# Feed-forward weight sums by VectorE and by accumulating transfers, and a fixed order for the last products, in a two-layer encoder trunk

## The chip, the cores and the metric

The kernel runs on one core of a Trainium2 chip. The metric is the device time of one execution in microseconds (us); lower is better. The shown time of a kernel is the median of several executions. A separate execution was taken with the hardware profiler; all rows below come from it.

## The reference

256 rows of 1024 channels (float32) pass through two layers. Each layer adds a half feed-forward, a mixer and another half feed-forward to the running rows `h`; the mixer is a convolution module in layer 0 and latent attention in layer 1. A final norm follows.

```
h += 0.5 * ((silu(n(h) @ w1) * (n(h) @ w3)) @ w2)     # n = RMSNorm; w1, w3: 1024 x 2816, w2: 2816 x 1024
h += mixer(n(h))                                      # layer 0: GLU, conv of width 31, norm, silu, product
h += 0.5 * ((silu(n(h) @ v1) * (n(h) @ v3)) @ v2)     # layer 1's mixer: low-rank q/k/v, rotary keys, softmax
```

So there are four feed-forwards, F0 to F3: two in the convolution layer and two in the attention layer. Each reads 33 MB of weights, and their products fill most of the time.

## The kernel before, in words

**Precision and weight blocks.** Products are made from pairs: a float32 matrix is split into a rounded high part `hi` and a remainder `lo`, and three matrix instructions (`mm3`: high x low, high x high, low x high) add up in PSUM. Weights come in blocks of 128 x 2048 (1 MB, one transfer on SyncE's queue into a `raw` buffer). For each block ScalarE writes `hi` (a cast) and VectorE writes `lo` (`raw - hi`), in two pieces of 1024 columns (`PIECES = 2`). There are four `raw` buffers and four `hi`/`lo` pairs, used in turn; a block may be cast once the pair's previous block has been used by TensorE. `weights()` hands out the next block and sees to it that the following ones are loaded ahead.

**A feed-forward.** `ffn_in` first makes the up-projection: six column groups c of 512 columns (the last is half as wide), 22 blocks. `turn` transposes each result through a DRAM buffer (`gd`, `gb`) and splits it into `Gh`, `Gl`. Then `Rows` makes the down-projection with 11 blocks ("units" 0 to 10) into four PSUM banks `o[tb, d]`: tb is the half of the rows (128 each), d the half of the 1024 columns. Units 0, 2, 4, 6 and 8 (`FAST`) are made by a Strassen-like scheme with 7 products in place of 8, so 21 matrix instructions in place of 24. It needs four sums of quarters of the weight block (`load_fast`: the first two by GpSimd at L172, two by VectorE at L173 and L174), which take a second `raw` buffer and a second `hi`/`lo` pair, and sums of quarters of the activations (`combine`: four subtractions by GpSimd, L611). Four of the seven products gather in shared banks p1, q6, p5, q7. After unit 8 `fold` adds these to `h`, with GpSimd doing the four additions to `h` (L552, L555, L557, L559). `finish` then takes units 9 and 10: per bank 12 matrix instructions, an addition of the bank to `h` (L566) and what the next stage can begin: `Plain` (in front of the convolution) or `Norm` (elsewhere) makes sums of squares on ScalarE (L298), a power on GpSimd, transposes on TensorE and the split of the normed rows into `Xh`, `Xl`. These two tiles lie idle from the end of an up-projection to the end of that feed-forward.

**What sets the order.** Every engine takes its instructions in a fixed order that a planner makes from a simulated timeline; instructions traced inside an `urgent` function go first, and `behind` puts a cast after the last six urgent instructions of its engine that were traced before it. In `finish` the last six products in front of the convolution wait, by an ordering (`after = nxt.turned`), behind the transposes of the first half of the rows; for `Norm` the list `turned` is empty.

Of the kernel before, what the change touches and what calls it, by code (L numbers as in the profile page):

```python
# [19 lines left out]
P = 128  # L20
D = 1024
# [24 lines left out]
FAST = (0, 2, 4, 6, 8)  # L46
# [34 lines left out]
def trunk(ctx: ExitStack, tc: tile.TileContext, x, xt, pos, invf, gains, gfin, wdw,  # L81
# [28 lines left out]
    for i in range(2):  # L110
        for w13, w2 in ((f1w13, f1w2), (f2w13, f2w2)):

            for cc_ in range(5):
                for m in range(2):
                    blocks += [w13[i, m, 2 * cc_ + a_] for a_ in range(2)]
            blocks += [w13[i, a_, 10] for a_ in range(2)]
            blocks += [("fast", w2[i, a_]) if a_ in FAST else w2[i, a_] for a_ in range(NF // 2)]
# [26 lines left out]
    def load(src, pieces=1):  # L144
        if isinstance(src, tuple) and src[0] == "fast":
            return load_fast(src[1])
# [12 lines left out]
        for i in range(pieces):  # L159
            c = slice(i * n // pieces, (i + 1) * n // pieces)  # L160
            behind(nc.scalar.copy(hi[:, c], raw[:, c]))  # L161
            behind(nc.vector.tensor_sub(lo[:, c], raw[:, c], hi[:, c].bitcast(F32)))  # L162
        return hi, lo

    def load_fast(src):

        raw = rawp.tile([P, HB], F32, tag="raw", name=uid("raw"))
        sums = rawp.tile([P, HB], F32, tag="raw", name=uid("sums"))
        nc.sync.dma_start(raw, src)
        v = raw.rearrange("p (b n) -> p b n", n=512)  # L170
        t = sums.rearrange("p (b n) -> p b n", n=512)
        behind(nc.gpsimd.tensor_tensor(t[:, 0:2, :], v[:, 0:4:3, :], v[:, 1:2, :].to_broadcast([P, 2, 512]), op=ALU.add))  # L172
        behind(nc.vector.tensor_add(t[:, 2, :], t[:, 0, :], v[:, 3, :]))  # L173
        behind(nc.vector.tensor_add(t[:, 3, :], t[:, 2, :], v[:, 2, :]))  # L174
        out = []
        for x, cols in ((raw, ((0, 512), (1024, 2048))), (sums, ((0, 1024), (1024, 2048)))):
            hi = wp.tile([P, HB], F32R, tag="hi", name=uid("hi"))
            lo = wp.tile([P, HB], F32R, tag="lo", name=uid("lo"))
            for c0, c1 in cols:
                behind(nc.scalar.copy(hi[:, c0:c1], x[:, c0:c1]))  # L180
                behind(nc.vector.tensor_sub(lo[:, c0:c1], x[:, c0:c1], hi[:, c0:c1].bitcast(F32)))  # L181
            out.append((hi, lo))
# [18 lines left out]
    def load_ahead(ahead=W_BUFS - 2):  # L201
# [4 lines left out]
        load_to(b)  # L206

    def load_to(last):
        while len(loaded) < last:
            loaded.append(load(blocks[len(loaded)], PIECES))  # L210

    def weights(n=1, more=True, ahead=W_BUFS - 2):
        out = []
        for _ in range(n):
            n_used[0] += 1
            if more:
                load_ahead(ahead)
# [117 lines left out]
    class Norm:  # L335


        def __init__(self, gname, half=False):
# [7 lines left out]
            self.turned = ()  # L346
# [152 lines left out]
    class Rows:  # L499
        def __init__(self, zh, zl, nk, last=False, sh=None, sl=None):  # L500
# [4 lines left out]
            self.early = max(i for i in range(nk // 2 - 2) if sh is None or i not in FAST)  # L505
# [6 lines left out]
        def mm(self, part, i, tb, d, o, key, f1, o0=0, o1=512, after=()):  # L512
            hi, lo = part
            for j in range(2):
                f = 2 * i + j
                c = slice(j * D + d * 512 + o0, j * D + d * 512 + o1)
                mm3(o, self.zh[:, f, tbs(tb)], self.zl[:, f, tbs(tb)], hi[:, c], lo[:, c], self.begin(key),
                    f == f1 - 1, after)
# [8 lines left out]
        def fast(self, i):  # L527

            n = FAST.index(i)
# [6 lines left out]
            for o, key, (ah, al), (hi, lo), q in (  # L536
                    (self.p[0], "p1", z(f, 0), raw, 0), (self.o[0, 0], (0, 0), z(f + 1, 0), raw, 2),
                    (self.o[0, 1], (0, 1), s(2), raw, 3), (self.p[2], "p5", z(f, 1), sums, 0),
                    (self.p[3], "q7", s(1), sums, 1), (self.p[1], "q6", s(0), sums, 2),
                    (self.o[1, 0], (1, 0), z(f + 1, 1), sums, 3)):  # L540
                c = slice(q * 512, q * 512 + 512)
                mm3(o, ah, al, hi[:, c], lo[:, c], self.begin(key), isinstance(key, str) and i == FAST[-1])
            if i == FAST[-1]:
                self.fold()

        def fold(self):
# [748 lines left out]
```

## Time and profile before

| | |
|---|---|
| median of 3 runs | 933.74 us (932.46 to 934.13) |
| profiled execution | 930.08 us, span 928.3 us |
| TensorE busy | 913.5 us (98%), clock 0.998 |
| VectorE / ScalarE / GpSimd busy | 687.6 / 536.4 / 213.4 us |
| DMA | 191.58 MB, mean 206 GB/s |

A profile row names a line, an engine, the operation and the tiles (`out<-in`), then how often it ran, its busy time, the mean of one and the idle time in front of it. In a timeline the first two columns are the start and the duration in us, and square brackets hold the idle time in front with what ended it. A windows view gives, for a stretch of time, its length and the busy time of TensorE, its weight loads, VectorE, ScalarE and GpSimd (instructions in brackets), then the clock, the DMA share and GB/s. PE is TensorE, DVE is VectorE, ACT is ScalarE, POOL is GpSimd, SP is SyncE.

### The profile page before, as it was taken

Reading aid. Unit: us, or ns where it says so; the run is one execution under the profiler, and the core shown is the slowest. Engines: PE = TensorE matmul, PEld = TensorE weight load, DVE = VectorE, ACT = ScalarE, POOL = GpSimd, SP = SyncE. Lnnn points to the kernel's source line nnn. Section 1 sums busy time; section 2 is a strip of 40 time slices with the busy share of each in tenths; the row PEclk is TensorE's granted clock in tenths of the full one; section 3 lists DMA queues with packets and bytes.
Section 4 is the critical chain, followed back from the end, with each engine's and each line's share of the span. In section 5 each row is a group of like instructions: output and inputs, shape, how many; then the busy total and the mean of one; then the engine's idle time right before and its main releaser. Section 6 shows DMA issues by size and latency. Waiting matters only on the chain.

```text
span 928.3 us, 12409 instructions
## 1 busy us (share of the span) xinstructions
PE 913.5 (98%) x4337; PEld 761.0 (82%) x4337; DVE 687.6 (74%) x1047; ACT 536.4 (58%) x928; POOL 213.4 (23%) x325
## 2 busy tenths in 40 slices
PE   9999999899999999999999999999999999999997
PEld 7888888798977888888888888888898778888886
DVE  5777787889974667778876667878666476667975
ACT  6964465558865445455575445655667374544643
POOL 1110222349931001222210003223200010003223
PEclk9999999999999999999999999999999999999999
DMA  9986555823323866565857765657451557774651
GB/s 340 348 291 231 203 170 216 317 90 139 137 91 127 299 243 237 184 196 198 308 198 237 246 233 184 193 206 262 181 182 46 182 204 236 254 246 150 226 181 46
DMA packets 60399, 191.58 MB, mean 206 GB/s; under 512 B 11184, under 2 KB 33328, under 8 KB 40752
## 3 DMA queue, kind: packets, MB, share of 16 engines
q1 hardware_dynamic: 59760, 190.09, 58.7%
q8 instruction: 34, 0.56, 0.2%
q10 hardware_dynamic: 576, 0.69, 0.2%
q14 instruction: 29, 0.24, 0.1%
HBM read 178.17 MB, written 12.58 MB: 205 GB/s over the span
## 4 chain that ended last, share of the span: by engine, by line
PE 89%; DVE 5%; ACT 3%; DMA 1%; issue 1%; SPq 0%; POOLq 0%; ACTq 0%; POOL 0%; DVEq 0%
PE u L275 17%; PE u L271 17%; PE u L274 17%; PE o L271 6%; PE o L274 6%; PE o L275 6%; DVE lo L162 3%; PE u L717 3%; PE gate L717 3%; PE p L275 2%; PE p L271 2%; PE p L274 2%; PE o L901 2%; PE y L790 2%; ACT hi L161 1%
## 5 line engine op out<-in xcount | busy, mean ns | idle before, releaser
L162 DVE TENSOR_TENSOR lo<-raw,hi 128x1024 fp32r<-128x1024 f32 (+1 forms) x250 | 304.9, 1255 | 76.9 <-ACT hi L161 76.8
L161 ACT CAST hi<-raw 128x1024 fp32r<-128x1024 f32 (+1 forms) x250 | 248.0, 1046 | 153.3 <-PE u L275 111.1
L275 PE MATMUL u<-hi,Xl 128*128 128x512 f32 x688 | 267.8, 390 | 0.7 <-DVE Xl L330 0.7
L271 PE MATMUL u<-lo,Xh 128*128 128x512 f32 x688 | 268.1, 390 | 0.1
L274 PE MATMUL u<-hi,Xh 128*128 128x512 f32 x688 | 267.7, 389 | 0.0
L275 PEld LDWEIGHTS u<-hi,Xl 128*128 128x128 f32 x688 | 129.2, 188 | 28.5 <-DVE Xl L330 1.6
L271 PEld LDWEIGHTS u<-lo,Xh 128*128 128x128 f32 x688 | 129.2, 188 | 26.8 <-DVE lo L162 0.5
L274 PEld LDWEIGHTS u<-hi,Xh 128*128 128x128 f32 x688 | 129.2, 188 | 26.8
L271 PE MATMUL o<-lo,Gh 128*128 128x512 f32 (+1 forms) x236 | 91.0, 386 | 0.0
L275 PE MATMUL o<-hi,Gl 128*128 128x512 f32 (+1 forms) x236 | 91.0, 385 | 0.0
L274 PE MATMUL o<-hi,Gh 128*128 128x512 f32 (+1 forms) x236 | 91.0, 385 | 0.0
L172 POOL TENSOR_TENSOR sums<-raw 128x1024 f32<-128x1024 f32 x20 | 53.1, 2653 | 161.2 <-DMA raw<-in_f2w 52.6
L611 POOL TENSOR_TENSOR sx<-gb 128x128 f32<-128x128 f32 x20 | 10.4, 521 | 311.9 <-DMA gb<-gd 311.9
L181 DVE TENSOR_TENSOR lo<-sums,hi 128x1024 fp32r<-128x1024 f32 x40 | 56.1, 1433 | 0.0
L603 ACT CAST Gh<-gb 128x512 fp32r<-128x512 f32 (+2 forms) x48 | 25.6, 539 | 49.8 <-DMA gb<-gd 49.6
L761 DVE SCALAR_TENSOR_TENSOR acc<-V,dw,acc 128x256 f32<-128x256 f32 (+1 forms) x160 | 54.0, 417 | 0.1
L180 ACT CAST hi<-sums 128x1024 fp32r<-128x1024 f32 x40 | 40.7, 1052 | 22.5 <-PE u L275 15.3
L604 DVE TENSOR_TENSOR Gl<-gb,Gh 128x512 fp32r<-128x512 f32 (+2 forms) x48 | 33.1, 704 | 26.4 <-ACT Gh L603 26.4
L275 PEld LDWEIGHTS o<-hi,Gl 128*128 128x128 f32 x236 | 44.3, 188 | 9.0
L274 PEld LDWEIGHTS o<-hi,Gh 128*128 128x128 f32 x236 | 44.3, 188 | 9.0
L271 PEld LDWEIGHTS o<-lo,Gh 128*128 128x128 f32 x236 | 44.3, 188 | 8.7
L180 ACT CAST hi<-raw 128x512 fp32r<-128x512 f32 (+1 forms) x40 | 31.4, 834 | 34.7 <-PE o L275 27.8
(246 smaller groups left out, 1336.6 us busy)
## 6 DMA issues: line engine op xcount, KB each, us to landing
raw<-in_f2w SPq DMA_DIRECT2D x66, 1024.0 KB, 4.8
raw<-in_f1w SPq DMA_DIRECT2D x64, 1024.0 KB, 5.3
raw<-in_cw SPq DMA_DIRECT2D x12, 1024.0 KB, 6.0
gd<-gt SPq DMA_DIRECT2D x160, 64.0 KB, 2.5
gb<-gd SPq DMA_DIRECT2D x40, 256.0 KB, 3.0
raw<-in_wo SPq DMA_DIRECT2D x4, 1024.0 KB, 4.9
raw<-in_wuq SPq DMA_DIRECT2D x3, 1024.0 KB, 4.7
raw<-in_f1w SPq DMA_DIRECT2D x8, 256.0 KB, 6.2
```

The source lines that it names most:

```text
L161: behind(nc.scalar.copy(hi[:, c], raw[:, c]))
L162: behind(nc.vector.tensor_sub(lo[:, c], raw[:, c], hi[:, c].bitcast(F32)))
L172: behind(nc.gpsimd.tensor_tensor(t[:, 0:2, :], v[:, 0:4:3, :], v[:, 1:2, :].to_broadcast([P, 2, 512]), op=ALU.add))
L180: behind(nc.scalar.copy(hi[:, c0:c1], x[:, c0:c1]))
L181: behind(nc.vector.tensor_sub(lo[:, c0:c1], x[:, c0:c1], hi[:, c0:c1].bitcast(F32)))
L271: mm = nc.tensor.matmul(o, ah, bl, start=start, stop=False)
L274: nc.tensor.matmul(o, ah, bh, start=False, stop=False)
L275: return nc.tensor.matmul(o, al, bh, start=False, stop=stop)
L603: nc.scalar.copy(dh, x)
L604: nc.vector.tensor_sub(dl, x, dh.bitcast(F32))
L717: mm = nc.tensor.matmul(u[:, t], w[:, c], X.x[:, k, t], start=(k == 0), stop=(k == KT - 1))
L761: nc.vector.scalar_tensor_tensor(out if j == j1 - 1 else y, v, w, y, op0=ALU.mult, op1=ALU.add)
```

## The change

- The weight blocks of a feed-forward other than those of its first column group are cast in one piece of 2048 columns ("wide"); fast blocks in pieces of 1536 (the quarter that is not used directly comes last in a new block layout) and 2048.
- The first two weight sums of units 0 and 2 go from GpSimd to one VectorE instruction. For units 4, 6 and 8 two transfers on GpSimd's queue make them: the last quarter is written twice, then the first two quarters are added by an accumulating transfer. They land in the space of `Xh` (units 4 and 8) and `Xl` (unit 6).
- `combine` goes to VectorE; the activation difference is made in place.
- `fold` is urgent and on VectorE; its half for the second rows is a new `fold_second`, traced after the second bank's addition. In unit 8 the four shared products come first.
- In `finish` the products have a fixed order (banks 0 and 1: unit 9 for both, then unit 10), each group behind the one before. The casts of the second block of the next stage are held until the second bank's addition has been traced (not in F0; in the attention's `finish` too). `Norm.turned` now holds the transposes of the first rows, so the last six products wait for them there as well.

```
-            blocks += [w13[i, a_, 10] for a_ in range(2)]
-            blocks += [("fast", w2[i, a_]) if a_ in FAST else w2[i, a_] for a_ in range(NF // 2)]
+                    blocks += [("wide", w13[i, m, 2 * cc_ + a_]) if cc_ else w13[i, m, 2 * cc_ + a_]
+                               for a_ in range(2)]
+            blocks += [("wide", w13[i, a_, 10]) for a_ in range(2)]
+            blocks += [("fast" if a_ in FAST[2 * i + g_] else "wide", w2[i, a_]) for a_ in range(NF // 2)]
...
+        casts() if later is None else later.append(casts)
...
+    def start_sums(b, tag):
+        src = blocks[b][1]
+        sums = xp.tile([P, HB], F32, tag=tag, name=uid("sums"))
+        t = sums[:, :1024].rearrange("p (b n) -> p b n", n=512)
+        nc.gpsimd.dma_start(t, src[:, 1536:].unsqueeze(1).to_broadcast([P, 2, 512]))
+        nc.gpsimd.dma_start(sums[:, :1024], src[:, :1024], accum_op=ALU.add)
+        sums_of[b] = sums
...
-        behind(nc.gpsimd.tensor_tensor(t[:, 0:2, :], v[:, 0:4:3, :], v[:, 1:2, :].to_broadcast([P, 2, 512]), op=ALU.add))
-        behind(nc.vector.tensor_add(t[:, 2, :], t[:, 0, :], v[:, 3, :]))
+        if sums is None:
+            sums = rawp.tile([P, HB], F32, tag="raw", name=uid("sums"))
+            t = sums.rearrange("p (b n) -> p b n", n=512)
+            nc.sync.dma_start(raw, src)
+            behind(nc.vector.tensor_add(t[:, 0:2, :], v[:, 0:2, :], v[:, 3:4, :].to_broadcast([P, 2, 512])))
+        else:
+            t = sums.rearrange("p (b n) -> p b n", n=512)
+            nc.sync.dma_start(raw[:, :1536], src[:, :1536])
+        behind(nc.vector.tensor_add(t[:, 2, :], t[:, 0, :], v[:, 1, :]))
         behind(nc.vector.tensor_add(t[:, 3, :], t[:, 2, :], v[:, 2, :]))
...
-        for x, cols in ((raw, ((0, 512), (1024, 2048))), (sums, ((0, 1024), (1024, 2048)))):
+        for x, n in ((raw, 1536), (sums, HB)):
...
         def part(self, tb, q, after=(), low_after=()):
             split_rows(h[tb], 4 * q, 4, self.col, self.xh, self.xl, tb, after, low_after,
-                       self.between if tb == 1 else None)
+                       self.between if tb == 1 else self.turned)
...
+            if end:
+                order_ = [shared[0], shared[3], shared[1], shared[2], *own]
+            else:
+                order_ = [shared[0], *own[:2], *shared[1:], own[2]]
...
+        @urgent
         def fold(self):
...
-            nc.gpsimd.tensor_tensor(h[0][:, left], h[0][:, left], s1, op=ALU.add)
...
+            nc.scalar.copy(s1, p1)
+            nc.vector.tensor_add(h[0][:, :512], p1, h[0][:, :512])
+            nc.vector.tensor_sub(self.v, q6, s1)
+            nc.vector.tensor_add(self.w, p5, self.v)
+            nc.vector.tensor_add(h[0][:, 512:], h[0][:, 512:], self.w)
+
+        @urgent
+        def fold_second(self):
+            for c, x, op in ((slice(0, 512), self.v, ALU.subtract), (slice(512, D), self.w, ALU.add)):
+                y = tmp.tile([P, 512], F32, tag="s", name=uid("fold"))
+                nc.vector.tensor_add(y, self.p[3], x)
+                nc.vector.tensor_tensor(h[1][:, c], h[1][:, c], y, op=op)
...
-            parts = weights(2)
+            later = []
+            parts = weights(1) + weights(1, later=later if hold else None)
...
+            steps = [(n, a) for n in range(len(pieces)) for a in range(2)]
+            if self.units:
+                steps[:4] = [(0, 0), (1, 0), (0, 1), (1, 1)]
+            before = None
+            for n, a in steps:
+                i, tb, d, o0, o1, o, key = pieces[n]
+                after = [before] if before is not None and self.units else []
+                if i == 3 and a == 1 and not self.last:
+                    after += nxt.turned
+                before = self.mm(parts[a], nb - 2 + a, tb, d, o, key, self.nk, o0, o1, after)
...
+                if i == 1:
+                    while later:
+                        later.pop()()
+                if i == 1 and self.units:
+                    self.fold_second()
...
-            sub(v[:, 3], b1[:, 0], b1[:, 1])
...
+                nc.vector.tensor_sub(s7, a21, a11)
+                nc.vector.tensor_sub(a21, a21, a22)
+                nc.vector.tensor_sub(s6, a11, a21)
+                nc.vector.tensor_sub(s3, a12, s6)
...
         for i in range(NF // 2 - 2):
-            (o.fast if i in FAST else o.block)(i)
+            for n, at, tag in ((2, 0, "Xh"), (3, 0, "Xl"), (4, units[2], "Xh")):
+                if i == at:
+                    start_sums(first_block + units[n], tag)
+            (o.fast if i in units else o.block)(i)
             beside()
-        return o.finish(make_next, act)
+        return o.finish(make_next, act, X.whole is False)
```

More of the change, by code (lines that the diff above doesn't have):

```diff
@@ L205, in load_ahead, with load_to, weights @@
             b += 1
-        load_to(b)
-    def load_to(last):
+        load_to(b, later)
+    def load_to(last, later=None):
         while len(loaded) < last:
-            loaded.append(load(blocks[len(loaded)], PIECES))
-    def weights(n=1, more=True, ahead=W_BUFS - 2):
+            loaded.append(load(blocks[len(loaded)], PIECES, later))
+    def weights(n=1, more=True, ahead=W_BUFS - 2, later=None):
         out = []
```

162 lines of the change are left out of this document (80 added, 82 removed).

## The prediction

> **What bounds the kernel now.** I read the page's busy shares, then the waits of TensorE, then windows around the places that these name. TensorE is busy 98% of the span; what it waits for is a list of single places.
>
> ```profile
> PE 913.5 (98%) x4337; PEld 761.0 (82%) x4337; DVE 687.6 (74%) x1047; ACT 536.4 (58%) x928; POOL 213.4 (23%) x325
> PE tp L433 <- ACT sigm L422: 2.9, 1, 2.9
> PE u L275 <- DVE Xl L330: 0.7, 2, 0.4
> 127.24 0.39 PE L271 MATMUL p<-lo,Gh 128*128 128x512 f32 x1
> 168.04 0.39 PE L271 MATMUL p<-lo,Gh 128*128 128x512 f32 x1
> 127.20:168.04 40.84, 40.84 (x181) 33.80 (x181) 34.31 (x37) 24.52 (x30) 10.55 (x7) 1.00 0.61 213
> 168.04:182.48 14.44, 14.44 (x64) 11.64 (x62) 13.13 (x12) 6.63 (x8) 6.42 (x4) 1.00 0.85 310
> 182.48:185.35 2.87, 0.00 (x1) 0.03 (x1) 1.16 (x3) 2.81 (x7) 1.40 (x4) 1.00 0.82 343
> 467.50:471.00 3.50, 3.22 (x21) 2.53 (x19) 1.82 (x5) 3.50 (x15) 1.97 (x7) 1.00 0.37 154
> ```
>
> The two matmul rows are the start of F0's down-projection (call it R) and of its unit 8 (T, 40.80 us later). Between them lie 4 fast units of 21 and 4 plain ones of 24: 180 instructions, 0.2267 us apart, so TensorE runs there without a gap, at full clock. Only at the end of F0, in front of the convolution, does it stand still: 2.87 us from 182.48. At the ends of F1 and F2 the loss is smaller, and is read from the starts of the first up-projection products (F1's are shown; F2's look alike):
>
> ```profile
> 468.80 0.48 PE L271 MATMUL u<-lo,Xh 128*128 128x512 f32 x1
> 469.12 0.40 PE L274 MATMUL u<-hi,Xh 128*128 128x512 f32 x1
> 469.79 0.51 PE L275 MATMUL u<-hi,Xl 128*128 128x512 f32 x1 [0.28 <-DVE Xl L330]
> 470.13 0.39 PE L271 MATMUL u<-lo,Xh 128*128 128x512 f32 x1
> ```
>
> Starts 0.32, 0.67 and 0.34 apart in place of 0.23: 0.65 us lost.
>
> **The change part by part.** Instructions of TensorE: none added or removed (five units of 21, six of 24 per feed-forward on both sides). So no work of the other engines counts unless TensorE waits for it, and the sum is one of stalls.
>
> *The end of F0 (gain).* Why does TensorE wait at 182.48? The additions to `h` are late, behind this queue of VectorE:
>
> ```profile
> 173.85 0.68 DVE L553 TENSOR_TENSOR fold<-p,fold 128x512 f32<-128x512 f32 x1
> 175.58 0.68 DVE L554 TENSOR_TENSOR fold<-p,fold 128x512 f32<-128x512 f32 x1
> 176.78 4.18 DVE L162 TENSOR_TENSOR lo<-raw,hi 128x1024 fp32r<-128x1024 f32 x2
> 180.88 0.68 DVE L558 TENSOR_TENSOR fold<-p,fold 128x512 f32<-128x512 f32 x1
> 181.48 1.87 DVE L566 TENSOR_TENSOR h<-o,h 128x512 f32<-128x512 f32 x3
> 182.25 0.63 ACT L298 ACTIVATE junk<-h 128x512 f32<-128x512 f32 x1 [7.24 <-DVE h L566]
> 183.00 0.63 ACT L298 ACTIVATE junk<-h 128x512 f32<-128x512 f32 x1
> 176.34 1.30 POOL L555 TENSOR_TENSOR h<-h,fold 128x512 f32<-128x512 f32 x1 [3.50 <-DVE fold L554]
> 177.60 2.28 POOL L557 TENSOR_TENSOR h<-h,fold 128x512 f32<-128x512 f32 x1
> 185.35 2.02 PE L433 MATMUL tp<-dR,h 128*128 128x128 f32 x16 [2.87 <-ACT sigm L422]
> ```
>
> The first bank's addition starts at 181.48 (T + 13.44), 3.87 us before the transposes at 185.35: 0.77 to the first squares, 0.75 to the second, another 0.75, and 1.60 for power and diagonal. It is that late because casts of later blocks stand between the steps of `fold` (4.18 us for two, slowed beside L557), and because GpSimd adds to `h`. After the change: unit 8's shared products end at T + 2.72 and its others at T + 4.76; bank 0 is whole 18 products later (T + 8.84), bank 1 at T + 10.20. `fold` takes a copy by ScalarE and four VectorE instructions of 0.68, 2.7 us; begun at T + 0.9, held up by the one wide `lo` of unit 10 (2.27, below), it ends near T + 6.4. `fold_second` (2.7 us) fits before T + 9.1, the addition of bank 0. Bank 1's addition begins at T + 10.4 and may sit behind one 1.21 us cast that has begun; with 0.77, 0.75 and 1.60 behind it the transposes can go at T + 13.5 to 14.7. TensorE has other products until T + 63 x 0.2267 = T + 14.28. So the 2.87 us fall to between 0 and 0.4; I take 2.6 gained, range 1 to 2.87.
>
> *Ends of F1 and F2 (gain).* The transposes now precede the last six products, 6 x 0.2267 = 1.36 us, under which the copies to `Xh` and `Xl` run. I take 0.5 of the 0.65 at each, 1.0 together; range 0 to 1.3.
>
> *The held casts (loss).* For F1 and F2 the second block is needed 2.72 us (12 products) after the next up-projection starts, and ScalarE has a gap after the first rows' `Xh` to cast in: nothing, or 1 us if it is missed. The attention's end has no such cover:
>
> ```profile
> 743.88 0.50 PE L271 MATMUL u<-lo,Xh 128*128 128x512 f32 x1
> 748.87 3.91 ACT L161 CAST hi<-raw 128x1024 fp32r<-128x1024 f32 x4
> 738.00:746.00 8.00, 7.47 (x38) 5.46 (x37) 4.03 (x9) 4.13 (x15) 1.16 (x4) 1.00 0.20 66
> ```
>
> Urgent work fills ScalarE until 748.87. A cast held back to there gives its first `lo` after 1.05 + 1.21 us, at 751.1; if TensorE takes all 24 products of the first block before it, it needs the second at 743.88 + 5.44 = 749.3. That is 1.8 us lost, against some 0.5 of the idle 0.53 that the earlier transposes win back. I take 0.6 lost; range 0.5 gained to 2 lost.
>
> *Casts, sums, `combine`, `fold` off the path.*
>
> ```profile
> L162 DVE TENSOR_TENSOR lo<-raw,hi 128x1024 fp32r<-128x1024 f32 x246 | 301.9, 1263 | 76.9 <-ACT hi L161 76.8
> L181 DVE TENSOR_TENSOR lo<-sums,hi 128x1024 fp32r<-128x1024 f32 x40 | 56.1, 1433 | 0.0
> L181 DVE TENSOR_TENSOR lo<-raw,hi 128x1024 fp32r<-128x1024 f32 x20 | 24.2, 1211 | 1.0 <-ACT hi L180 1.0
> L181 DVE TENSOR_TENSOR lo<-raw,hi 128x512 fp32r<-128x512 f32 x20 | 13.7, 684 | 4.9 <-ACT hi L180 4.9
> L180 ACT CAST hi<-raw 128x1024 fp32r<-128x1024 f32 x20 | 21.0, 1049 | 0.0
> L180 ACT CAST hi<-raw 128x512 fp32r<-128x512 f32 x20 | 12.4, 619 | 34.7 <-PE o L275 27.8 <-issue 5.8 <-DVE lo L162 1.0
> L172 POOL TENSOR_TENSOR sums<-raw 128x1024 f32<-128x1024 f32 x20 | 53.1, 2653 | 161.2 <-DMA raw<-in_f2w 52.6 <-DMA gd<-gt 36.8 <-DMA raw<-in_f1w 32.3
> DVE sums L173 <- POOL sums L172: 32.8, 16, 3.0
> L604 DVE TENSOR_TENSOR Gl<-sx,Gh 128x128 fp32r<-128x128 f32 x20 | 10.4, 518 | 0.0
> L604 DVE TENSOR_TENSOR Gl<-gb,Gh 128x384 fp32r<-128x384 f32 x20 | 15.7, 787 | 25.4 <-ACT Gh L603 25.4
> L604 DVE TENSOR_TENSOR Gl<-gb,Gh 128x512 fp32r<-128x512 f32 x20 | 14.8, 738 | 1.0 <-ACT Gh L603 1.0
> L840 DVE TENSOR_TENSOR Zl<-Z,Zh 128x128 fp32r<-128x128 f32 x8 | 2.2, 290 | 1.5 <-ACT Zh L839 1.4
> ```
>
> From 684 and 1211 ns a wide `lo` is an estimated 1.211 + 2 x 0.527 = 2.27 us, one of 1536 columns 1.74; on ScalarE 1.91 and 1.48. A plain block's last `lo` comes 4.2 us after its cast may start, against 3.5 now. A pair's turn-round in the down-projection is one fast and one plain unit, 4.76 + 5.44 = 10.2 us, so 6 us of cover remain; in the up-projection three blocks, 16 us. Throughput of VectorE per 10.2 us: with its own sums 1.21 + 1.37 + 1.74 + 2.27 + 2.27 = 8.9, with transferred ones 7.7. Its load before was 34.31 in 40.84 us. `combine` adds 4 x 0.29 per fast unit, and one split of 512 columns in place of two saves 0.518 + 0.787 - 0.738 = 0.57: 0.6 more each, spread over 22 us of up-projection. Two things also leave: waits behind GpSimd (32.8 us in all) and slow instructions beside it (1433 against 1211 ns). All this I cost at nothing. Should VectorE's cover go, each us of lateness of a `lo` costs one.
>
> *The transfers on GpSimd's queue.* No accumulating transfer is in the trace. The nearest are others of 512 KB:
>
> ```profile
> h<-in_x SPq DMA_DIRECT2D x2, 512.0 KB, 9.4
> gf<-in_gfin SPq DMA_DIRECT2D x1, 512.0 KB, 3.7
> ```
>
> Two in a row: 7.4 to 18.8 us. The first pair may start at R, when the up-projection lets `Xh` go. Behind it wait 1.37 + 1.91 + 2.27 = 5.6 us of sums and casts, and unit 4 needs them at R + 20.4 + 2.0: the pair must land by R + 16.8. GpSimd's queue makes the second pair wait for the first; unit 6 gives it until R + 27, unit 8 gives the third until R + 36. So a pair may take 12 us before TensorE waits. I take the 3.7 row, 7.4 a pair, no cost: the 9.4 is of loads queued among the first weights, and R lies in a stretch with a DMA share of 0.61; behind them GpSimd has no other work in this stage. The unused quarter spares 0.25 MB per `raw` load, on SyncE's queue.
>
> **Sum.** 2.6 + 1.0 - 0.6 = 3.0 us less than the profiled 930.08: 927.1. The median of the runs is 3.66 above that execution, so 930.7.
>
> **The rivals.**
>
> *The held casts decide (other side, slower).* If TensorE's order takes the first rows' twelve products of the first block and then wants the second block, the attention's end loses 751.1 - 746.6 = 4.5 us, and F1 and F2, where the gap is missed, 1 us each in place of their gains. From 2.6 gained to 6.5 lost: 3.9 us slower, 937.6. It decides from a lateness of 3.6 us in all, the size of the gains. For it: ScalarE's unbroken urgent work up to 748.87. Against: at F1's end TensorE's products already go on in another order where an operand is late.
>
> *Late transfers.* At 15 us a pair the second lands at R + 30, 3 late, the third 6 later still: 9 us in each of four feed-forwards, less 3.0: 966. For it: the 9.4 row. Against: R lies in a calm stretch.
> If each transfer's issue also waits for one VectorE instruction, at most 2.27 us, a pair of 7.4 becomes 7.4 + 4.5 = 11.9: the margin to 12 is gone, though TensorE does not wait yet and the time stays 930.7. So this rival has 0.08, and not less. The Trainium skill, "SBUF — State Buffer", section "Who interferes with whom", has such a rule: a VectorE instruction in a two-port mode holds the port that GpSimd needs, and GpSimd blocks for the whole instruction; no run here shows a transfer issued by GpSimd.
>
> *The stall at F0's end stays.* In F0 the casts are not held; two of them ahead of bank 1's addition and one ahead of bank 0's give 2 us of the 2.6 back: 932.7, no change.
>
> **How the numbers follow.** Forecast 0.60; its own range is 929.1 (2.87 + 1.3 + 0.5 gained) to 932.2 (half of the gains). Held casts 0.20, late transfers 0.08, stall stays 0.12. 0.2% of 933.74 is 1.9 us, about what a measurement of this kernel can tell from no change: faster is under 931.9. The forecast's case lies there for 0.55 and within 0.2% for 0.05; held casts are slower for 0.17, within for 0.03; late transfers slower; the third within for 0.09, faster for 0.03. Faster 0.58, same 0.17, slower 0.25. The range starts 1.1 below 929.1, for the spread of runs (932.46 was 1.3 under the median), and ends at 938, behind the held casts' 937.6; it leaves out the late transfers and some of the held casts' tail.
>
> **What would show it.** Right: no TensorE wait in front of the transposes at F0's end, L433 starting right behind products; VectorE without waits on GpSimd; the down-projection still at 40.8 us from R to T; L566's first addition near T + 9. Wrong: TensorE waiting for `lo` or `hi` in the down-projection (late transfers, VectorE's order stuck on sums) or in the first column group after the attention; a first addition later than T + 11.

## The result, and the profile after

The changed kernel takes 948.79 us (median of 4 runs, 947.51 to 949.55) against 933.93 us (4 runs, 932.46 to 934.68) for the kernel before on the same chip: a ratio of 1.016, 95% interval 1.0142 to 1.0177. It is 14.9 us slower; forecast were 930.7 us and a range of 928 to 938. Its profiled execution took 947.51 us with a span of 945.7 us, 17.4 us more than the span of before.

TensorE's instructions are the same 4337. Here are the head of the page after, and rows of its waits (us in total, times, longest):

```profile
span 945.7 us, 12055 instructions
PE 921.0 (97%) x4337; PEld 765.6 (81%) x4337; DVE 683.3 (72%) x995; ACT 518.2 (55%) x772; POOL 106.6 (11%) x233
```

```profile
ACT Gh L652 <- DMA gb<-gd: 45.0, 14, 8.8
DVE Gl L653 <- ACT Gh L652: 23.8, 7, 5.9
PE p L292 <- DVE lo L202: 11.6, 5, 4.0
PE tp L454 <- DVE dR L448: 1.7, 1, 1.7
```

The wait at F0's end went from 2.87 to 1.71 us. New are waits of a `p` product for `lo`, 11.6 us in all: one in unit 4 of every feed-forward (3.98, 2.25, 2.08 and 3.04 us), before its first product that needs `sums`, and a fifth of 0.19. Unit 4 is the first with transferred sums. TensorE's timeline of the kernel after around the one in F1:

```profile
438.75 0.39 PE L296 MATMUL o<-hi,Sl 128*128 128x512 f32 x1
441.39 0.50 PE L292 MATMUL p<-lo,Gh 128*128 128x512 f32 x1 [2.25 <-DVE lo L202]
...
442.88 0.63 PE L296 MATMUL p<-hi,Sl 128*128 128x512 f32 x1
443.31 0.63 PE L292 MATMUL p<-lo,Sh 128*128 128x512 f32 x1
```

The products behind the wait start 0.43 us apart in place of 0.23. In the windows the last three figures are the granted clock, the DMA share and GB/s:

```profile
442.00:444.00 2.00, 2.00 (x7) 1.60 (x6) 2.00 (x3) 2.00 (x2) 0.51 (x1) 0.60 0.39 135
444.00:446.00 2.00, 2.00 (x6) 1.54 (x6) 2.00 (x2) 0.29 (x1) 0.00 (x0) 0.55 0.96 291
```

Behind the four waits 13, 9, 8 and 9 products run at that pace and lose 2.75, 1.70, 1.65 and 1.67 us. So the four waits, 11.35 us, cost 11.35 + 7.77 = 19.1 us. Against them stand 1.2 us gained at F0's end and 0.5 to 0.7 us at the start of each stage behind F1, F2 and the attention (1.75 together, from first product to first product). That makes 16.2 of the 17.4 us; the rest lies in gaps too small to name.

Who is late? F1's down-projection starts at R = 416.54. First SyncE's queue, then VectorE's and ScalarE's timelines of the kernel after:

```profile
424.14 0.35 SPq L161 DMA_DIRECT2D raw<-in_f2w  x1
424.64 0.35 SPq L681 DMA_DIRECT2D gb<-gd  x1
425.04 0.92 SPq L194 DMA_DIRECT2D raw<-in_f2w  x1
426.13 0.39 SPq L681 DMA_DIRECT2D gb<-gd  x1
```

```profile
430.17 0.68 DVE L195 TENSOR_TENSOR sums<-sums,raw 128x512 f32<-128x512 f32 x1
435.91 0.42 DVE L653 TENSOR_TENSOR Gl<-gb,Gh 128x256 fp32r<-128x256 f32 x1 [5.06 <-ACT Gh L652]
436.26 0.68 DVE L196 TENSOR_TENSOR sums<-sums,raw 128x512 f32<-128x512 f32 x1
437.46 0.69 DVE L195 TENSOR_TENSOR sums<-sums,raw 128x512 f32<-128x512 f32 x1 [0.52 <-DMA raw<-in_f2w]
438.19 0.69 DVE L196 TENSOR_TENSOR sums<-sums,raw 128x512 f32<-128x512 f32 x1
439.04 2.29 DVE L202 TENSOR_TENSOR lo<-sums,hi 128x2048 fp32r<-128x2048 f32 x1 [0.16 <-ACT hi L201]
```

```profile
435.47 0.41 ACT L652 CAST Gh<-gb 128x256 fp32r<-128x256 f32 x1 [7.01 <-DMA gb<-gd]
437.10 1.91 ACT L201 CAST hi<-sums 128x2048 fp32r<-128x2048 f32 x1 [1.21 <-DVE sums L196]
```

Unit 4's sums have landed by 430.17, where VectorE adds to them. But the next two instructions in ScalarE's and VectorE's queues split the last column group of the up-projection, which TensorE needs only in unit 10. Its `gb` was issued at 424.64 and is there at 435.47. Unit 4's second addition (436.26), the two additions for unit 6, its cast and its `lo` (439.04) come behind. The groups of DMA issues give the time from issue to landing of these small loads, before and after:

```profile
gb<-gd SPq DMA_DIRECT2D x8, 128.0 KB, 2.1
```

```profile
gb<-gd SPq DMA_DIRECT2D x8, 128.0 KB, 10.7
```

And the DMA engines in the 24 us from R - 2 of F1: the row of the window (share, GB/s at its end) and the queues (packets, MB, share of 16 engines), first of the kernel after, then of e1, the same kernel without transferred sums:

```profile
414.54:438.54 24.00, 24.00 (x108) 19.88 (x107) 15.56 (x21) 9.94 (x10) 3.39 (x4) 1.00 0.97 310
q0 software_dynamic: 576, 2.10, 37.2%
```

```profile
408.78:432.78 24.00, 24.00 (x108) 19.87 (x107) 21.16 (x24) 13.87 (x13) 0.00 (x0) 1.00 0.66 228
```

Without the pairs the engines are busy 66% of this time; 0.34 x 24 = 8.2 us are free. The two pairs started at R take 0.372 x 24 = 8.9 us. They fill it. SyncE's order is another one too: in e1 both loads of `gb` are issued ahead of the large loads of `raw`, here a load of `raw` stands ahead of them. Load and order both make `gb` late: 2.0 us in e1, 5.8 with all transfers and `gb` first (e9 of the next section), 6.7 with one pair in place of three and `raw` first (e10), 10.7 with all transfers and `raw` first.

### The profile page after: what moved, and what is told of

Its sections match the earlier page's. It is cut to its first block, busy times and chain, and to the rows that moved or that the text cites. A ratio compares the mean times of both kernels' runs of the same rounds, so it can differ in the third digit from the quotient of the medians.

```text
span 945.7 us, 12055 instructions
## 1 busy us (share of the span) xinstructions
PE 921.0 (97%) x4337; PEld 765.6 (81%) x4337; DVE 683.3 (72%) x995; ACT 518.2 (55%) x772; POOL 106.6 (11%) x233
## 4 chain that ended last, share of the span: by engine, by line
PE 57%; DMA 23%; DVE 10%; ACT 5%; issue 3%; SPq 2%; POOL 0%; DVEq 0%; POOLq 0%; ACTq 0%
PE u L292 10%; PE u L295 10%; PE u L296 9%; DMA gb<-gd 8%; DMA gd<-gt 5%; DVE lo L167 5%; PE o L292 3%; PE o L295 3%; DMA sums<-in_f1w 3%; PE o L296 3%; DMA raw<-in_f1w 3%; PE u L770 3%; PE gate L770 3%; ACT hi L166 3%; DMA raw<-in_f2w 2%
## 5 line engine op out<-in xcount | busy, mean ns | idle before, releaser
L167 DVE TENSOR_TENSOR lo<-raw,hi 128x2048 fp32r<-128x2048 f32 (+2 forms) x154 | 285.4, 1874 | 86.1 <-ACT hi L166 82.6
L166 ACT CAST hi<-raw 128x2048 fp32r<-128x2048 f32 (+2 forms) x154 | 239.5, 1589 | 172.2 <-PE u L296 130.2
L652 ACT CAST Gh<-gb 128x512 fp32r<-128x512 f32 (+1 forms) x48 | 28.0, 583 | 66.4 <-DMA gb<-gd 45.0
L201 ACT CAST hi<-sums 128x2048 fp32r<-128x2048 f32 x20 | 38.2, 1909 | 39.1 <-DVE sums L196 24.1
L653 DVE TENSOR_TENSOR Gl<-gb,Gh 128x512 fp32r<-128x512 f32 (+1 forms) x48 | 30.8, 641 | 23.8 <-ACT Gh L652 23.8
L832 ACT ACTIVATE prod<-V,dw 128x128 f32<-128x128 f32 (+1 forms) x121 | 45.9, 420 | 3.6 <-POOL Y L833 1.8
L202 DVE TENSOR_TENSOR lo<-sums,hi 128x2048 fp32r<-128x2048 f32 x20 | 45.6, 2281 | 2.4 <-ACT hi L201 2.2
L201 ACT CAST hi<-raw 128x1536 fp32r<-128x1536 f32 x20 | 29.6, 1478 | 28.8 <-PE o L296 23.5
L202 DVE TENSOR_TENSOR lo<-raw,hi 128x1536 fp32r<-128x1536 f32 x20 | 35.1, 1753 | 7.7 <-ACT hi L201 7.7
```

Source lines behind the costliest of these rows:

```text
L201: behind(nc.scalar.copy(hi[:, :n], x[:, :n]))
L202: behind(nc.vector.tensor_sub(lo[:, :n], x[:, :n], hi[:, :n].bitcast(F32)))
L652: nc.scalar.copy(dh, x)
L653: nc.vector.tensor_sub(dl, x, dh.bitcast(F32))
L832: nc.scalar.activation(p, v, AF.Copy, scale=w)
```

## The experiments

**e1: are the transfers the source?**

```
-            for n, at, tag in ((2, 0, "Xh"), (3, 0, "Xl"), (4, units[2], "Xh")):
-                if i == at:
-                    start_sums(first_block + units[n], tag)
```

> Edit: no accumulating transfer at all, VectorE makes the sums of all five units of each feed-forward; everything else of the change stays. Three theories put the loss on the transfers: (clog) their traffic at the start of the down-projection keeps the DMA engines busy at a low rate, so the last two small loads of gb land some 9 us late and ScalarE, whose fixed order has their casts ahead of those of the sums, stands; (order) SyncE's queue now has large loads of raw ahead of those loads of gb; (late sums) the sums themselves land too late for unit 4. All three expect the stall in unit 4 to go, gb back to about 2 to 4 us, and 926 to 931 us, that is the 933.9 of before less the 3 to 7 us that the profile after shows gained at F0's end, F1, F2 and the attention's end. The rival (casts: the wide casts, held casts or VectorE's extra work make the weights late) expects the stall to stay or grow, since VectorE has 1.2 us more to do per unit: 945 to 955.

Measured: 927.61 us, ratio 0.995 (0.993 to 0.996). The stalls in unit 4 and the slow products behind them are gone, `gb` lands in 2.0 us, and VectorE's added work costs little: in the down-projections there are only two waits, both in F0.

```profile
139.74 0.50 PE L292 MATMUL p<-lo,Gh 128*128 128x512 f32 x1 [0.33 <-DVE lo L202]
143.01 0.50 PE L292 MATMUL o<-lo,Gh 128*128 128x512 f32 x1 [0.25 <-DVE lo L167]
```

With the slower starts around them they cost 1.1 us (F0's R to T takes 42.0 us there, 40.8 in the other three). The whole loss hangs on the transfers, and the rest of the change is a gain.

**e3: does the accumulation matter, or only the bytes?**

```
-        nc.gpsimd.dma_start(sums[:, :1024], src[:, :1024], accum_op=ALU.add)
+        nc.gpsimd.dma_start(sums[:, :1024], src[:, :1024])
```

> Edit: the second transfer of each pair is a plain copy instead of an accumulating one (same bytes, same queue, same time of start); the addition of the fourth quarter is left out of the sums of units 4, 6 and 8, so the output is not the reference's. (clog), if it is the accumulation that is slow, expects 928 to 934 and DMA engines that move over 300 GB/s in the 20 us from the start of the down-projection. (order) expects no change: about 949, gb still at some 11 us. (late sums) expects something between, as the pair lands earlier by what the accumulation costs: 931 to 940.

Measured: 932.45 us, ratio 1.000 (0.998 to 1.002). The same window around F1's R, of e3:

```profile
409.64:433.64 24.00, 24.00 (x108) 19.87 (x107) 17.11 (x22) 11.55 (x11) 2.66 (x4) 1.00 0.91 327
q0 software_dynamic: 576, 2.10, 25.7%
```

The same 2.10 MB take 0.257 x 24 = 6.2 us of all engines, 3.1 us for each half. With accumulation it was 8.9, so the accumulating half took an estimated 5.8 us, 1.9 times as long (taking the two halves of e3 as equal). `gb` still lands late (8.2 us, from R + 15.7 to R + 17.9 in place of R + 18.8 to R + 20.7), and waits of 1.18, 0.54 and 1.46 us remain, too short for slow products. VectorE's order is that of the kernel after. So accumulation is worth 16.3 us of the kernel's time, though `gb` is only 2 to 3 us earlier without it: the waits get short, and short ones are not followed by slow products.

**e4: are the sums late, or are full engines enough?**

```
-            for n, at, tag in ((2, 0, "Xh"), (3, 0, "Xl"), (4, units[2], "Xh")):
+            for n, at, tag in ((3, 0, "Xh"), (4, 0, "Xl")):
```

> Edit: only units 6 and 8 have transferred sums, both pairs started at the start of the down-projection; VectorE makes unit 4's, and its load of raw takes two buffers again, by which SyncE's order comes out with gb ahead of the next load. (late sums) expects the stall to go, since unit 6 has 10 us more than unit 4 had: 928 to 933. (order) expects the same, 928 to 933, with gb at 2 to 4 us. (clog) expects gb still 7 us or more from its issue, because two pairs start at the same moment as in the kernel after, ScalarE's wait on it, the stall in unit 4 and 940 to 949.

Measured: 928.13 us, ratio 0.995 (0.993 to 0.997). The DMA share of the window is 0.95, as high as in the kernel after, `gb` takes 6.5 us and ScalarE waits up to 9.6 us for it, yet TensorE waits at most 0.30 us in unit 4. Full engines by themselves do not cost time: theory (clog) in the form expected is wrong. In VectorE's queue the additions to unit 6's sums came out behind unit 4's `lo` here; e13 shows what that is worth.

**e2, e5, e9: SyncE's order.** Each puts loads of `raw` behind the last loads of `gb` (the last line shown is e9's; e2 and e5 begin two units earlier in three feed-forwards):

```
+    def behind_back(dma):
+        if len(loaded) >= backs[1]:
+            order(dma, backs[0].ins)
...
-            nc.sync.dma_start(raw[:, :1536], src[:, :1536])
+            behind_back(nc.sync.dma_start(raw[:, :1536], src[:, :1536]))
...
+        backs[1] = first_block + 5
```

> Edit: the kernel after, with its transfers, but SyncE issues both last loads of gb ahead of the load of raw that now stands before or between them. (order) expects gb to land within 2 to 4 us of its issue, ScalarE's 7 to 9 us wait to go, no stall in unit 4 and 928 to 933 us. (clog) expects gb to take still 7 us or more from issue, since the accumulating transfers have the DMA engines anyway, and 943 to 949. (late sums) expects ScalarE's wait on gb to go but VectorE's wait on sums to grow by as much, and 943 to 949.

> Edit: as e2_gb_first, but the order ends with each down-projection. In e2 it ran on into the next up-projections, whose loads of raw then waited for transfers of gb, and only its first feed-forward tests what was meant: there gb landed 16.5 us after the start of the down-projection in place of 20.7, and TensorE waited 0.2 us before unit 4's first sums product in place of 4.0. (order) expects this in all four: 930 to 934 us. (clog), by which the accumulating transfers alone are enough, expects gb still at 18.8 us or later in the other three, and 940 to 949.

> Edit: the kernel after, with its transfers; only the loads of raw of units 5 and later stand behind both last loads of gb in SyncE's queue, as in the kernel before. (e5 had put those of units 3 and 4 behind them too in three of the four feed-forwards, and TensorE then waited 5.9 to 7.9 us for unit 3's weights; its first feed-forward alone had this edit, and the wait before unit 4's first sums product was 0.8 + 0.3 us there in place of 4.0.) If SyncE's order is what makes the full DMA engines hurt, unit 4's stall falls under 1 us in all four and the time is 929 to 935 us. If full DMA engines (97% in the 24 us around the start of the down-projection) are enough by themselves, another late load takes the place of gb, as in e6, and the time stays at 942 to 950.

Measured: e2 1055.6 us (ratio 1.133, 1.128 to 1.138), e5 958.2 us (1.027, 1.024 to 1.031), e9 931.87 us (1.000, 0.998 to 1.003). e2 and e5 missed: their edits reached too far. In e2 the order ran on into the up-projections, in e5 it held back the loads of units 3 and 4 in three feed-forwards, and TensorE waited there (19.8 us for three `lo` of unit 3). Only e9 makes the edit that was meant. No stall in unit 4 is left, although the DMA engines are 91 to 98% busy in the 24 us from R - 2; one of 1.50 us is in F1's unit 8. But e9 changed more than SyncE's queue: the program that orders VectorE's instructions placed unit 6's additions behind unit 4's `lo` this time:

```profile
429.69 2.29 DVE L207 TENSOR_TENSOR lo<-sums,hi 128x2048 fp32r<-128x2048 f32 x1 [0.55 <-ACT hi L206]
431.91 0.69 DVE L200 TENSOR_TENSOR sums<-sums,raw 128x512 f32<-128x512 f32 x1
```

**e6: the last column group's split out of the way.** SyncE's order as in the kernel after; the split stands behind unit 4's casts on both engines:

```
-            split(gh, gl, bv)
+            if c < 5:
+                split(gh, gl, bv)
+            else:
+                last_splits.append(lambda casts: split(gh, gl, bv, casts))
...
+            if i == 4:
+                while last_splits:
+                    last_splits.pop(0)(casts_of[first_block + 4])
```

> Edit: the kernel after with all its transfers and SyncE's order; only the split of the last column group (Gh on ScalarE, Gl on VectorE) stands behind unit 4's casts in their queues, and not ahead of them. If the stall comes from the fixed order of ScalarE and VectorE, which have the late gb ahead of work that is ready, it goes and the time is 928 to 934 us, with gb as late as in the kernel after (18.8 to 20.7 us from the start of the down-projection). If unit 4's sums land too late themselves, VectorE waits on sums at that place instead, TensorE stalls as before, and the time is 943 to 949.

Measured: 950.02 us, ratio 1.018 (1.016 to 1.021); neither theory's reason. VectorE's timeline of e6 in F2:

```profile
615.27 0.69 DVE L197 TENSOR_TENSOR sums<-sums,raw 128x512 f32<-128x512 f32 x1
621.93 0.69 DVE L196 TENSOR_TENSOR sums<-sums,raw 128x512 f32<-128x512 f32 x1 [5.96 <-DMA raw<-in_f1w]
622.66 0.69 DVE L197 TENSOR_TENSOR sums<-sums,raw 128x512 f32<-128x512 f32 x1
623.27 2.28 DVE L203 TENSOR_TENSOR lo<-sums,hi 128x2048 fp32r<-128x2048 f32 x1
```

Unit 4's sums are whole at 615.96 and their `hi` at 618.03, but the `lo` (623.27) stands behind the additions for unit 6, and these wait 5.96 us for unit 6's load of `raw`. Taking the first late operand out of the queue showed the second, which in the kernel after was hidden behind it (0.52 us at 437.46).

**e13, e14: which order decides?** e13 is e6 with unit 6's additions behind unit 4's `lo`; e14 is e9 with them ahead:

```
+            if len(loaded) - 2 in casts_of:
+                order(ins, casts_of[len(loaded) - 2][1].ins)
...
+        if len(loaded) == backs[1] + 1:
+            order(lows[len(loaded) - 2], added[1].ins)
```

> Edit: e6_split_late (all transfers, SyncE's order of the kernel after, the last column group's split behind unit 4's casts), and VectorE's additions for unit 6's sums stand behind unit 4's lo too. In e6 they stood ahead of it and waited 3.4 to 6.3 us for unit 6's load of raw. If the loss is late landings held against ready work by the fixed order of VectorE and ScalarE, nothing late stands ahead of unit 4's lo any more, its stall falls under 1 us and the time is 928 to 935 us, though SyncE's order and the DMA engines' load are those of the kernel after. If the full DMA engines or SyncE's order are enough by themselves, the next late operand stalls TensorE (unit 5's or unit 6's weights) and the time stays over 940.

> Edit: e9_gb_first_only, but VectorE's additions for unit 6's sums stand ahead of unit 4's lo again, as in the kernel after (in e9 they had come out behind it). If SyncE's order alone made e9's gain, the time is e9's: 930 to 934. If VectorE's order is needed as well, unit 4's lo waits for unit 6's load of raw, which lands about 21 us after the start of the down-projection, TensorE waits 2 to 4 us in each feed-forward, runs at the slow pace behind it, and the time is 940 to 949.

Measured: e13 931.12 us, ratio 0.998 (0.996 to 0.999); e14 954.03 us, 1.022 (1.020 to 1.025), more than expected, since unit 8 and F0's end (3.27 us) lose too. VectorE in F1, first e13, then e14:

```profile
428.28 2.29 DVE L207 TENSOR_TENSOR lo<-sums,hi 128x2048 fp32r<-128x2048 f32 x1 [2.10 <-ACT hi L206]
433.51 0.69 DVE L196 TENSOR_TENSOR sums<-sums,raw 128x512 f32<-128x512 f32 x1 [2.94 <-DMA raw<-in_f2w]
```

```profile
442.02 0.69 DVE L201 TENSOR_TENSOR sums<-sums,raw 128x512 f32<-128x512 f32 x1 [3.55 <-DMA raw<-in_f2w]
442.75 0.69 DVE L202 TENSOR_TENSOR sums<-sums,raw 128x512 f32<-128x512 f32 x1
443.36 2.28 DVE L210 TENSOR_TENSOR lo<-sums,hi 128x2048 fp32r<-128x2048 f32 x1
```

The same load is waited for in both. In e13 unit 4's `lo` is done by then, and in the down-projections TensorE waits at most 0.62 us at a time; in e14 it comes behind. The four combinations:

| | unit 6's additions ahead of unit 4's `lo` | behind it |
|---|---|---|
| SyncE: `raw` ahead of `gb` | 948.79 (after), 950.02 (e6) | 931.12 (e13) |
| SyncE: `gb` first | 954.03 (e14) | 931.87 (e9) |

VectorE's order decides, SyncE's does not: with late data at the head of VectorE's queue the kernel takes some 18 to 22 us more, whichever load is late. By their edits e6 and e13 differ in that order alone. The right-hand column still takes about 4 us more than e1 (ratios 0.998 and 1.000 in place of 0.995). Part of that is the third pair, unit 8's: it lands at R + 37.2 in e9's F1, and TensorE waits 1.50 us for it there; in e13 it lands at R + 36.2 to R + 36.7 in three feed-forwards, with waits of 0.41 to 0.62 us. F0's end waits 1.9 us in both. (In e13 the split is out of unit 4's way too; in e9 it stands ahead, but its first `gb` lands at R + 13.0 to R + 14.6.)

**e10: half of the load.**

```
-            for n, at, tag in ((2, 0, "Xh"), (3, 0, "Xl"), (4, units[2], "Xh")):
+            for n, at, tag in ((2, 0, "Xh"),):
```

> Edit: only unit 4 has transferred sums, started at the same moment as in the kernel after; VectorE makes those of units 6 and 8. SyncE's order still has one large load of raw ahead of both loads of gb. If the DMA engines' capacity decides, the one pair brings half of the 8.9 us of work that two pairs bring into 24 us of which 8.2 were free, the engines have pauses again, gb lands within 5 us of its issue, there is no stall and the time is 926 to 931. If sums by transfer are too late for unit 4 in any case, or if the one large load ahead of gb is enough, the stall of 2 to 4 us stays in each feed-forward: 938 to 949.

Measured: 929.36 us, ratio 0.998 (0.995 to 1.000). The DMA share of F1's window is 0.77, one wait of 1.31 us is left in F1's unit 4, none in the others. `gb` takes 6.7 us, not under 5 as expected, and costs nothing. So transferred sums are in time for unit 4 where the engines have room.

**e7: why do products run slowly behind the wait?**

```
+                for _ in range(FILL if n == 2 and key == "p5" else 0):
+                    zeros.append(nc.tensor.matmul(o[:, :256], still[:, :P], still, start=False, stop=False))
```

> Edit: the kernel after with 16 products of zeros (128x256, bf16) in front of unit 4's first sums product, in each feed-forward, some 1.8 us of TensorE work inside a wait of 2.1 to 4.0 us; they add zero to an open bank. Theory (idle): TensorE's products run 0.427 us apart in place of 0.227 for 3 to 6 us after the stall because TensorE stood idle; with the zeros at most 0.3 to 2.2 us are idle, the 7.9 us lost behind the four stalls go in whole or most, and the time is 941 to 944. Rival (the slow products come from something else at that place, such as traffic or late weights): no change, 947 to 950. Both keep the stall itself, since sums come no earlier.

Measured: 968.92 us, ratio 1.039 (1.036 to 1.042), far from both; but the question is answered at its place. TensorE of e7 in F0:

```profile
149.54 1.92 PE L574 MATMUL p<-still 128*128 128x256 bf16 x16
152.46 0.50 PE L293 MATMUL p<-lo,Gh 128*128 128x512 f32 x1 [0.99 <-DVE lo L203]
152.79 0.40 PE L296 MATMUL p<-hi,Gh 128*128 128x512 f32 x1
```

The clock stays at 1.00 for the next 4 us (0.50 at that place in the kernel after). In F2, where 1.78 us of waiting are left behind the zeros, nine slow products follow. Idle time was the cause of the slow products. The time is lost 18 us later, in unit 7, by rows of its waits:

```profile
DVE sums L196 <- DMA sums<-in_f1w: 16.9, 2, 8.5
PE o L293 <- DVE lo L168: 18.3, 4, 5.2
```

VectorE had, in this kernel's order, the additions to unit 8's sums ahead of unit 7's `lo`, and they waited 8.4 us for the third pair: the same pattern once more, with a third operand.

**e8, e11, e12, e15: what the rest of the change is worth.** All four are e1 with one or two further edits: casts held at F0's end too (e8), casts in two pieces again (e11), no fixed order of the last products, which also frees the last six from waiting for the transposes of a `Norm` (e12), e8 with e11 (e15):

```
-        return o.finish(make_next, act, X.whole is False)
+        return o.finish(make_next, act)
...
-            src, pieces = src[1], 1
+            src = src[1]
...
-                steps[:4] = [(0, 0), (1, 0), (0, 1), (1, 1)]
...
-                after = [before] if before is not None and self.units else []
-                if i == 3 and a == 1 and not self.last:
+                after = []
+                if i == 3 and a == 1 and isinstance(nxt, Plain):
```

> Edit: e1_all_vector with the second block's casts held at the end of the first feed-forward too. In e1 four casts of 1024 columns (4.63 us) still stand ahead of the first addition to h there, and TensorE waits 1.50 us before the transposes. If these casts set that wait, two of the four go behind the additions, 1 to 1.5 us are gained and the time is 926 to 927. If ScalarE's squares and table load or the second rows set it, the time stays at 927.6; if the held block is wanted earlier than that, it is 928 to 930.

> Edit: e1_all_vector with the casts of plain and fast blocks in two pieces again, as before the change. If the wide casts cost and bring nothing, as the prediction has it, the time is e1's: 926.5 to 928.5 (0.993 to 0.996 of the kernel before). If their later last lo costs TensorE something, narrow ones give under 926; if fewer instructions bring something, over 929.

> Edit: e1_all_vector without the fixed order of the last products, the transposes of the next stage free to stand anywhere, as before the change; casts held as in the change. If the fixed order gives the gain at the ends of F1 and F2 (0.55 us each) and part of F0's, the time rises by 1 to 3 us, to 928.5 to 930.5; if it is the holding of the casts and VectorE's additions that give it, the time stays at 926.5 to 928.5.

> Edit: e8_all_vector_hold with the casts in two pieces of e11_all_vector_narrow: no transfers, VectorE's sums, fixed order, held casts in every feed-forward. e8 gained 1.9 us and e11 1.3 us on e1; both take from the same wait at F0's end (1.50 in e1, none in e8, 0.70 in e11), so they do not add in full: 924 to 926 us, 0.991 to 0.993 of the kernel before. If the pieces help elsewhere too, 924.

Measured: e8 925.74 us (ratio 0.993, 0.991 to 0.995), e11 926.27 (0.993, 0.991 to 0.994), e12 931.21 (0.998, 0.997 to 0.999; a little more than expected), e15 925.50 (0.992, 0.989 to 0.994). e8 and e11 overlap with e1 by their ratios; what they do is seen in VectorE's timeline at F0's end, first of e1, then of e8:

```profile
176.14 4.63 DVE L167 TENSOR_TENSOR lo<-raw,hi 128x1024 fp32r<-128x1024 f32 x4
180.68 1.29 DVE L598 TENSOR_TENSOR h<-o,h 128x512 f32<-128x512 f32 x2
```

```profile
175.44 2.35 DVE L167 TENSOR_TENSOR lo<-raw,hi 128x1024 fp32r<-128x1024 f32 x2
177.71 0.69 DVE L598 TENSOR_TENSOR h<-o,h 128x512 f32<-128x512 f32 x1
```

With two casts fewer ahead of the additions the wait before the transposes, 1.50 us in e1, is gone; in e11 it is 0.70. The two small waits of e1 in F0 are not in e8 either, so its span is 2.5 us shorter. Without the fixed order (e12) the waits for `Xl` at the start of the stages behind F1 and F2 (0.27 us each) and behind the attention (0.42) are back, and these three stages take 0.7, 0.7 and 1.1 us longer than in e1. e15 is the fastest kernel here, 0.8% faster than before; whether it is faster than e8 and e11 these runs can't tell.

## Why the prediction was wrong

**The step that failed** is "the transfers on GpSimd's queue", taken at "7.4 a pair, no cost". Its size was wrong. The row taken has 3.7 us for 512 KB; those of the kernel after, and GpSimd's timeline of F1, have:

```profile
sums<-in_f1w POOLq DMA_DIRECT2D x12, 512.0 KB, 7.3
sums<-in_f2w POOLq DMA_DIRECT2D x12, 512.0 KB, 5.9
417.17 1.59 POOL L179 DMA_DIRECT2D sums<-in_f2w  x2 [118.03 <-PE u L296]
422.93 0.93 POOL L180 DMA_DIRECT2D sums<-in_f2w  x1 [4.18 <-DMA sums<-in_f2w]
424.25 0.87 POOL L180 DMA_DIRECT2D sums<-in_f2w  x1 [0.38 <-DMA sums<-in_f2w]
```

The second pair does not wait for the first, as I had it: the first halves of both are issued together (417.17), and they run side by side. From its first issue to its last landing a pair takes 11 to 19 us in place of 7.4, near the 15 of the rival. The two accumulating halves alone take an estimated 5.8 us of all engines. And "R lies in a calm stretch" was read from a share over 40 us (0.61); the pairs needed 8.9 us in 24 us with 8.2 free.

The deadlines were about right. Unit 4's sums kept theirs, R + 16.8: in F1 VectorE found them there at R + 13.6 (after), and waited for them until R + 11.9 (e9), R + 13.5 (e14) and, once past the deadline, R + 17.6 (e6). The third pair missed its R + 36: it can start only when unit 4's `lo` has freed `Xh`, which the prediction left out, at R + 25.1 to R + 27.0 in the kernel after, and lands at R + 39.6 to R + 42.1. There TensorE is itself 4 to 7 us late by then (R to T takes 44.7 to 47.7 us in place of 40.8) and does not wait for it.

What was left out altogether is what full engines do to the *other* transfers issued at that time (`gb`, the load of unit 6), and who stands behind those. The prediction asked what is late for the sums, not what the sums make late. The Trainium skill has the rule that was missing, in "DMA: Bandwidth & Descriptors", section "Issuing engines are not separate DMA queues": transfers of every issuing engine run on the same 16 DMA engines and interleave. The rows agree: with GpSimd's pairs on the engines SyncE's small loads take 5.8 us in place of 2.0 where they are issued first (e9, e1), and 10.7 behind a load of `raw`. The prediction's list of signs had "TensorE waiting for `lo` ... VectorE's order stuck on sums"; VectorE was stuck on `gb` and `raw`, with sums that had landed. The rival "late transfers" (chance 0.08, 966 us) is the nearest, with the wrong operand.

**Casts, sums, `combine`, `fold` at nothing:** nearly right. In e1, where all of them stay, the two waits for `lo` in F0 (0.33 and 0.25 us) cost 1.1 us with the slower starts around them; e8, with the same sums, has neither. The sentence "each us of lateness of a `lo` costs one" was too cheap: 11.35 us of waiting cost 19.1, 1.7 each, by the slow products.

**F0's end, 2.6 gained:** in e1 1.37 (2.87 to 1.50), in the kernel after 1.16. The term was mis-sized by the casts: I put the first addition at T + 9.1 with no cast of the next stage ahead of it, and let one of 1.21 us stand ahead of the second; in e1 four stand ahead of both (4.63 us), and the first starts at 180.68, T + 11.7. Where two are held back (e8) it starts at T + 9.4 and nothing waits. The mechanism was right, and so was the rival on this stall as to where the gain went, though not in the number of casts.

**Ends of F1 and F2, 1.0 gained:** right, 1.05 us by the lengths of the stages behind them. Both waits are gone in the kernel after. They are back in e12, which leaves out the fixed order and, for a `Norm`, the ordering behind the transposes; which of the two removes them no run separates.

**Held casts, 0.6 lost:** wrong in sign. From the first product behind the attention to the last down-projection the kernel after takes 120.3 us, before 121.0: 0.7 gained, beyond the good end of the range (0.5), and none of the 1.8 us lost shows. The rival built on it, 937.6, did not come.

**The sum:** without the transfers it comes close, in part by luck. The prediction's 927.1 for a profiled execution is 928.35 in e1, 925.88 in e8. In e1 F0's end gains 1.2 us less than forecast, the held casts' stage 1.3 more, and the two waits in F0 cost 1.1: together 2.0 us gained in place of 3.0, as the spans have it (928.3 and 926.3).

**A blocked port:** the rule that the prediction cites from the Trainium skill ("SBUF — State Buffer", section "Who interferes with whom") shows nowhere: GpSimd's 24 issues took 0.74 to 0.97 us each.

## What to carry to other kernels

Before you add transfers in idle time, work out the DMA engines' free time in the very window where they start, and then list every other transfer issued there and what stands behind its first reader on each engine. A late operand costs nothing until a ready and urgent instruction stands behind it in an engine's queue; then take the late reader out of the way, or start less. Where one late operand is removed, look for the next one behind it: here three different ones gave the same stall.

## What was unexpected

- **Accumulating transfers are dear.** 1.05 MB took an estimated 5.8 us of all 16 DMA engines, a plain copy of the same bytes 3.1 us (windows of the kernel after and e3).
- **A 128 KB load takes up to five times as long beside them:** 10.7 us in place of 2.1 behind a 1 MB load of its own queue, 5.8 us ahead of it (e9).
- **Short waits halve the clock.** Over all runs here, a wait in front of a 128x512 product of split parts was followed by at most two slow products up to 1.60 us of idle time, and by 6 to 14 of them, 1.4 to 2.9 us lost, from 1.76 us on, unless the next wait came sooner (twice in e2). The convolution's products of unsplit float32 are another matter: they run 0.43 us apart at a clock of 1.00. At F0's end, where transposes follow, it is less clear: 2.87 us in the kernel before were followed by none, 1.89 in e6 by 1.6 us lost. The Trainium skill, "TensorE: Matmul & The Clock Gate", section "Part 1: The HAM clock gate", has the half clock after an idle window of about 3.4 us and the full one after about as long a busy time, with windows that run freely. The pace (0.427 us for 512 columns) agrees; half of that idle time was enough here.
- **VectorE's queue keeps its order even where its head waits 6 us for a load and an instruction behind it is ready** (e6: from 615.96 to 621.93, with unit 4's `lo` ready from 618.03). The Trainium skill, "PSUM — Partial Sum Buffer", section "Engine vs sequencer instructions", says that the queues of ScalarE, VectorE and GpSimd are strictly first in, first out; these rows agree.
